# Attention heads with the gated branch's output products held behind their scores, two tiles a head, and the next head's loads written ahead

## The chip, the cores and the metric

The kernel runs on one core of one Trainium2 chip. Its time is device time in microseconds (us). A core has TensorE (PE, matrix products; its weight loads are shown apart as PEld), VectorE (DVE), ScalarE (ACT), GpSimd (POOL) and SyncE (SP), whose queue issues the kernel's transfers here. Each works through its own instructions in order, and they wait for each other by semaphores.

## What is computed

One decoder block on x of 1024 rows by 1024 columns, float32: half of the mixing width is attention with a forget gate in 8 heads of 64, the other half a gated branch in chunks of 128 rows; both go through one output matrix, then comes a gated feed-forward with a short convolution.

```
q, k, v, u, vg, f = split(rmsnorm(x) @ w_in)
logits = q @ k.T / 8 + c_i - c_j          # c: running sum of log sigmoid(f), causal
att = softmax(logits) @ v                  # 8 heads of 64
sg = u * (tril(w_s) @ rmsnorm(vg) + b_s)   # u, vg after gelu; 8 groups of 64, chunks of 128 rows
h = x + concat(att, sg) @ w_out
h = h + conv_ffn(rmsnorm(h))               # 1024 -> 2 x 2816 -> 1024, convolution of width 3
out = rmsnorm(h)
```

## The kernel before, in words

Products are made in float32r with each operand split into a high and a low part, so that one product of matrices is three on TensorE (high by high, high by low, low by high). The stages follow each other: input projections, attention, the output matrix, the up projection, the down projection. The program is written out in full; a scheduler then sets the order of each engine's instructions. It takes, of those that are ready by its own reckoning, the one that stands first in the program, and gives out buffers (each tag has a fixed number of them) as they come free. A helper, `after`, adds an order between two instructions of one engine without a wait. So the place of a piece in the program is its rank, and not its time.

The attention runs over 8 heads (`att_head`). A head loads five blocks into two tiles: A (queries, high and low part), B and B2 (keys, and the keys with their parts swapped), and nck, the forget sums laid over all partitions (L706 to L710). Tags "x1" and "x2" have two buffers, so a head's loads need the buffers of the head before the last. Then come four steps `i` of two query tiles `j` of 128 rows. For each `j` POOL forms the bias t (L725), TensorE the scores in "s" banks of PSUM (L733, L734, and the causal mask L736 on the diagonal), DVE adds both and takes the least (L738), ACT takes the exponent (L741). After the two `j` come as many tiles of the gated branch's products as `FILLS` says for this step, by `next(filler)`. Then the step's weights are transposed (L755), split in two by ACT and DVE (L756, L757) and multiplied with the values (L765). At the head's end its row sums are transposed (L777), stored and read back over 64 partitions (L779, L780). After each second head, POOL scales the pair's result and ACT and POOL split it into attT (L786 to L788); the third and the fourth pair's attT lie in "G" buffers.

The generator `sg_out` makes the gated branch's part of the output matrix: for each half of 512 columns it loads and splits four blocks of rows into the four "whl" buffers (L796 to L799), then, for each of 8 tiles of 128 rows, it loads x, makes twelve products of 128x512 into one bank (L808 to L810), adds x on DVE (L811) and stores the sum to hpd (L812). That is 16 tiles of twelve. Its left operands sgT fill all four "G" buffers until the last tile is done. The tiles' x and the raw weights share four "raw" buffers.

`wo_load` stands before the last head in the program. It loads the attention's four blocks of rows of the output matrix (L822) and splits them on ACT and POOL (L157 and L163 within `split_w`): the first two into the "whl" buffers, the other two into "G". After the heads come those rows' products (L906 to L908) and, with loads L865 and L881 into "raw" and sums on POOL (L884 to L887), the first weights of the up projection.

Of the kernel before, what the change touches and what calls it, by code (L numbers as in the profile page):

```python
# [16 lines left out]
BIG = 3.0e38  # L17
NFF = 22
WARM = 11
FILLS = [1, 2] * 10 + [2] + [0] * 11  # L20
FCFG = ("b", 4, 4)


# [35 lines left out]
def after(tc, later, earlier):  # L59
    tc.add_manual_dep(later.ins, earlier.ins.name, mybir.DependencyInfo(  # L60
        mybir.DependencyClass.NoSync, mybir.DependencyReason.DATA), reason="order")
# [3 lines left out]
def block_kernel(ctx: ExitStack, tc: tile.TileContext, xT, xtok, wuv, wv, wqk, wf, cpk, bfv,  # L65
                 ggain, g2r, gfr, wsp, woa, wos, wup, wdn, out):
    nc = tc.nc
    act, dve, pool, pe, sp = Line(nc.scalar, tc), Line(nc.vector, tc), Line(nc.gpsimd, tc), nc.tensor, nc.sync
# [6 lines left out]
    drm = ctx.enter_context(tc.tile_pool(name="drm", bufs=1, space=bass.MemoryType.DRAM))  # L75
    FILL = FILLS
    FTAG, FB, BB = FCFG
# [4 lines left out]
    def nm(s):  # L82
        uid[0] += 1
        return f"{s}_{uid[0]}"
# [18 lines left out]
    def f32(ap):  # L103
        return ap.bitcast(F32)
# [165 lines left out]
    B = [bank() for _ in range(4)]  # L270
# [61 lines left out]
    B, S = S, B  # L332
# [5 lines left out]
    for j in range(2):  # L338
        t1, t2, t3 = tmp[j]
        for c in range(2):  # L340
            k = 2 * j + c
# [27 lines left out]
    for j in range(2):  # L369
        t2 = tmp[j][1]  # L370
        for c in range(2):
            k = 2 * j + c
# [253 lines left out]
    for hf in (1, 0):  # L626
        for c in range(4):
            src = vgt[hf][:, :, c * P:(c + 1) * P].rearrange("p t (g d) -> p g t d", g=2)
            h = vgs[c][:, 0, :, hf * 4:hf * 4 + 4, :]
# [22 lines left out]
    sgT = [None] * 4  # L652
# [44 lines left out]
    attT = [None] * 4  # L697
    attF = [None] * 4

    TTAG = ["t01", "t01", "t2", "t3"]  # L700

    def att_head(h, order=(0, 1, 2, 3)):
        p, hh = h // 2, h % 2
        ab, nb = sb("x1", [P, 2, 1024], F32R), sb("x2", [P, 2, 1024], F32R)
        A, B, nck, B2 = ab[:, 0, :], ab[:, 1, :], f32(nb[:, 0, :]), nb[:, 1, :]
        sp.dma_start(out=f32(A), in_=qd[h].rearrange("s d t -> (s d) t"))  # L706
        sp.dma_start(out=f32(B), in_=kd[h].rearrange("s d t -> (s d) t"))
        sp.dma_start(out=nck, in_=ncd[h:h + 1, :].to_broadcast((P, 1024)))
        sp.dma_start(out=f32(B2[0:64, :]), in_=kd[h, 1])
        sp.dma_start(out=f32(B2[64:128, :]), in_=kd[h, 0])  # L710
        if hh == 0:
            attF[p] = sb("H", [P, 2, 1024])
        rs = sml.tile([P, 8], F32, tag="rs", name=nm("rs"))
        po = None
        tlow = sb("H", [P, 10 * P])
        for i in order:
            w1, w2 = (2 * i + 1) * P, (2 * i + 2) * P
            tp = tlow[:, 3 * i * P:3 * i * P + w1 + w2] if i < 2 else sb(TTAG[i], [P, w1 + w2])
            tj = (tp[:, 0:w1], tp[:, w1:w1 + w2])
            for jj in range(2):  # L720
                j = 2 * i + jj
                n = (j + 1) * P
                qs = slice(j * P, (j + 1) * P)
                t = tj[jj]
                pool.tensor_scalar(out=t, in0=nck[:, 0:n], scalar1=-1.0, scalar2=ncq[:, h, j:j + 1],  # L725
                                   op0=ALU.mult, op1=ALU.add)
                mn = sml.tile([P, 2], F32, tag="mn", name=nm("mn"))
                lo_ = lim[:, 0:1]
                for c in range(0, n, 512):
                    e = min(n, c + 512)  # L730
                    last = e == n
                    ps = sbank()
                    pe.matmul(ps[:, 0:e - c], A[:, qs], B[:, c:e], start=True, stop=False)  # L733
                    pe.matmul(ps[:, 0:e - c], A[:, qs], B2[:, c:e], start=False, stop=not last)  # L734
                    if last:
                        pe.matmul(ps[:, e - c - P:e - c], identb, maskb, start=False, stop=True)  # L736
                    m = mn[:, c // 512:c // 512 + 1]
                    dve.tensor_tensor_reduce(out=t[:, c:e], in0=ps[:, 0:e - c], in1=t[:, c:e], scale=1.0,  # L738
                                             scalar=lo_, op0=ALU.add, op1=ALU.min, accum_out=m)
                    lo_ = m  # L740
                act.activation(t, t, AF.Exp, bias=lo_, scale=-1.0, accum_out=rs[:, j:j + 1])  # L741
            for _ in range(FILL[4 * h + list(order).index(i)]):
                next(filler, None)
            if i % 2 == 0:
                po = bank()
            oc = (i % 2) * 256
            for k0 in range(0, 2 * i + 2, 2):
                pt = sb("pt", [P, 2, 512], F32R)
                ptr = bank()
                diag = k0 == 2 * i  # L750
                blocks = [(k0, 0, 0), (k0, 1, 128)] + ([(k0 + 1, 1, 256)] if diag else
                                                      [(k0 + 1, 0, 256), (k0 + 1, 1, 384)])
                w = 384 if diag else 512
                for k, jj, c in blocks:
                    pe.transpose(ptr[:, c:c + P], tj[jj][:, k * P:(k + 1) * P], ident)  # L755
                act.copy(pt[:, 0, 0:w], ptr[:, 0:w])  # L756
                dve.tensor_tensor(out=pt[:, 1, 0:w], in0=ptr[:, 0:w], in1=f32(pt[:, 0, 0:w]), op=ALU.subtract)  # L757
                for k in (k0, k0 + 1):
                    lhs = V[k // 2][:, k % 2, h, :, :].rearrange("p s d -> p (s d)")
                    half = k == 2 * i + 1  # L760
                    o = (k - k0) * 256
                    n = 128 if half else 256
                    oo = oc + (128 if half else 0)
                    for s in range(2):
                        pe.matmul(po[:, oo:oo + n], lhs, pt[:, s, o:o + n], start=(k == 0 and s == 0),  # L765
                                  stop=(s == 1 and half))
            if i % 2 == 1:
                hf = i // 2
                o = slice(hf * 512, hf * 512 + 512)
                r = slice(hh * 64, hh * 64 + 64)  # L770
                act.copy(attF[p][r, 0, o], po[64:128, :])
                dve.tensor_tensor(out=attF[p][r, 0, o], in0=po[0:64, :], in1=attF[p][r, 0, o], op=ALU.add)

        ptr = bank()
        rt = sb("t01", [8, P])
        dve.reciprocal(rs, rs)
        pe.transpose(ptr[0:8, 0:P], rs, ident)  # L777
        act.copy(rt, ptr[0:8, 0:P])
        sp.dma_start(out=rsd[h], in_=rt)  # L779
        sp.dma_start(out=attF[p][hh * 64:hh * 64 + 64, 1, :],  # L780
                     in_=rsd[h].rearrange("a b -> (a b)").unsqueeze(0).to_broadcast((64, 1024)))
        if hh == 1:
            attT[p] = sb("A" if p < 2 else "G", [P, 2, 1024], F32R)
            f = attF[p]
            for o, eng in (((slice(0, 1024), pool),) if p < 3 else ((slice(0, 512), dve), (slice(512, 1024), dve))):
                eng.tensor_tensor(out=f[:, 0, o], in0=f[:, 0, o], in1=f[:, 1, o], op=ALU.mult)  # L786
                act.copy(attT[p][:, 0, o], f[:, 0, o])
                eng.tensor_tensor(out=attT[p][:, 1, o], in0=f[:, 0, o], in1=f32(attT[p][:, 0, o]), op=ALU.subtract)  # L788

    def sg_out():  # L790
        for hf in range(2):
            o = slice(hf * 512, hf * 512 + 512)
            whs = []
            for kp in range(2):
                wr = sb("raw", [P, 2, 512])
                sp.dma_start(out=wr, in_=wos[hf, kp])  # L796
                for j in range(2):
                    w = sb("whl", [P, 2, 512], F32R)
                    split_w(wr[:, j, :], (w[:, 0], w[:, 1]), "act", "pool")  # L799
                    whs.append(w)  # L800
            for tt in range(8):
                ts_ = slice(tt * P, (tt + 1) * P)
                hs = sb("raw", [P, 512])
                sp.dma_start(out=hs, in_=xtok[ts_, o])
                ps = fbank()
                for k in range(4):
                    w = whs[k]
                    pe.matmul(ps, sgT[k][:, 0, ts_], w[:, 0, :], start=(k == 0), stop=False)  # L808
                    pe.matmul(ps, sgT[k][:, 0, ts_], w[:, 1, :], start=False, stop=False)  # L809
                    pe.matmul(ps, sgT[k][:, 1, ts_], w[:, 0, :], start=False, stop=(k == 3))  # L810
                dve.tensor_tensor(out=hs, in0=ps, in1=hs, op=ALU.add)  # L811
                sp.dma_start(out=hpd[tt, :, o], in_=hs)  # L812
                yield
# [5 lines left out]
    def wo_load():  # L819
        for k in range(4):  # L820
# [9 lines left out]
                w = [t[:, :, hf * 512:hf * 512 + 512] for hf in range(2)]  # L830
            wo.append(w)

    for h in range(8):
        if h == 7:
            for _ in filler:
                pass
            wo_load()
        att_head(h)


    ss2 = cst.tile([P, 8], F32, name="ss2")
# [129 lines left out]
    for tt in (0, 4, 1, 5, 2, 6, 3, 7):  # L971
        hload(tt)
        for hf in range(2):
# [3 lines left out]
            else:  # L977
                ps = bank()
# [29 lines left out]
    for i in range(AHEAD):  # L1008
# [4 lines left out]
        if i == 0:  # L1013

            last = flip(7)
# [311 lines left out]
```

## Time and profile before

| | |
|---|---|
| time, median of 3 runs | 1108.23 us (1107.27 to 1109.26) |
| the profiled execution's own time | 1112.15 us |
| its span, first to last instruction | 1110.4 us |
| granted TensorE clock, mean | 0.991 |
| busy: PE, DVE, ACT, POOL | 1079.6, 900.5, 572.3, 262.9 us |
| scores of head 0, first (L733) | at 226.5 us |
| gated branch's products (L808), first and last | at 233.1 and 314.2 us |
| first product of the attention's output rows (L906) | at 401.9 us |

A row of the profile names the engine, the line, what is written and read, how often, and how long. Line numbers are those of the kernel before. The clock is the share of full speed that TensorE was granted. A wait is put down to the instruction that ended it.

### The profile page before, as it was taken

What the parts mean: (1) busy time and instruction counts of PE and PEld (TensorE: products, weight loads), DVE (VectorE), ACT (ScalarE), POOL (GpSimd) and SP (SyncE); (2) the same over time, 40 slices, a digit from 0 to 9 for tenths busy, and PEclk for the clock granted to TensorE, in tenths of its full rate; (3) what the DMA queues carried; (4) which work ended last, traced back from release to release, by engine and by line L of the source; (5) the groups of instructions that cost most, each with busy time, mean ns of one, the idle gap of its engine ahead of it and who ended that gap; (6) DMA issues with size and microseconds to landing.
All of it is one profiled execution on the core that took longest, in us unless ns stands there. A gap on an engine that the chain in (4) does not pass through costs nothing.

```text
span 1110.4 us, 14553 instructions
## 1 busy us (share of the span) xinstructions
PE 1079.6 (97%) x5077; PEld 885.0 (80%) x5077; DVE 900.5 (81%) x1357; ACT 572.3 (52%) x990; POOL 262.9 (24%) x205
## 2 busy tenths in 40 slices
PE   9999998999998999998999999999999999999997
PEld 6888787787887788777788888888888888888886
DVE  5985799775668867799899999989898875898774
ACT  5656543454476775644444444353444445444653
POOL 0002233133245450243333332333242000000000
PEclk9999999999998999999999999999999999999999
DMA  9242356836575325322323133222321799433342
GB/s 339 82 152 77 97 165 175 256 126 216 188 210 165 105 100 185 114 72 81 114 95 123 67 123 114 95 96 104 133 80 54 254 321 333 135 95 96 125 139 97
DMA packets 64714, 158.19 MB, mean 142 GB/s; under 512 B 7672, under 2 KB 7936, under 8 KB 64640
## 3 DMA queue, kind: packets, MB, share of 16 engines
q1 hardware_dynamic: 64480, 156.73, 42.3%
q8 instruction: 40, 0.66, 0.2%
q10 hardware_dynamic: 160, 0.53, 0.1%
q14 instruction: 34, 0.28, 0.1%
HBM read 114.95 MB, written 42.27 MB: 142 GB/s over the span
## 4 chain that ended last, share of the span: by engine, by line
PE 68%; DVE 7%; ACT 3%; issue 2%; POOL 2%; DMA 1%; SPq 0%; ACTq 0%; DVEq 0%; POOLq 0%
PE k L1184 18%; PE qc L999 9%; PE qd L999 9%; PE qa L999 9%; PE qb L999 4%; PE pb L765 3%; PE ps L260 2%; PE pb L755 2%; PE pf L808 1%; PE pf L809 1%; PE pf L810 1%; DMA x<-ncd 1%; PE pb L906 1%; PE pb L908 1%; PE pb L907 1%
## 5 line engine op out<-in xcount | busy, mean ns | idle before, releaser
L1184 PE MATMUL k<-whb,wha 128*128 128x512 f32 x924 | 209.7, 389 | 0.0
L1184 PEld LDWEIGHTS k<-whb,wha 128*128 128x128 f32 x924 | 173.4, 188 | 36.1
L999 PE MATMUL qc<-xT,whb 128*128 128x512 f32 x540 | 132.0, 393 | 5.2 <-ACT cg L1078 3.1
L999 PE MATMUL qa<-xB,wha 128*128 128x512 f32 x528 | 127.2, 390 | 1.8 <-ACT xB L947 1.2
L999 PEld LDWEIGHTS qc<-xT,whb 128*128 128x128 f32 x540 | 102.2, 190 | 28.0 <-ACT cg L1078 3.5
L999 PEld LDWEIGHTS qa<-xB,wha 128*128 128x128 f32 x528 | 98.9, 188 | 22.7 <-ACT xB L947 1.5
L157 ACT CAST wha<-sg 128x512 fp32r<-128x512 f32 x77 | 47.9, 622 | 97.5 <-PE k L1184 85.5
L157 ACT CAST whb<-sg 128x512 fp32r<-128x512 f32 x88 | 53.8, 617 | 77.1 <-PE qc L999 70.0
L163 DVE TENSOR_TENSOR wha<-sg,wha 128x512 fp32r<-128x512 f32 x77 | 52.8, 688 | 42.1 <-ACT wha L157 41.9
L163 DVE TENSOR_TENSOR whb<-sg,whb 128x512 fp32r<-128x512 f32 x88 | 66.6, 759 | 9.4 <-ACT whb L157 9.3
L999 PE MATMUL qd<-xT,whb 128*128 128x512 f32 x264 | 63.7, 389 | 1.9 <-DVE u L1061 1.9
L999 PE MATMUL qd<-xB,whb 128*128 128x512 f32 x264 | 63.5, 390 | 0.4 <-DVE h L1071 0.4
L765 PE MATMUL pb<-pt,V 128*128 128x256 f32 (+1 forms) x320 | 59.8, 302 | 3.8 <-ACT pt L756 3.2
L756 ACT CAST pt<-pb 128x512 fp32r<-128x512 f32 (+1 forms) x80 | 41.2, 544 | 40.0 <-PE pb L755 39.5
L999 PE MATMUL qb<-xT,whb 128*128 128x512 f32 x252 | 61.0, 390 | 0.0
L885 POOL TENSOR_TENSOR sg<-sg,raw 128x512 f32<-128x512 f32 x22 | 44.0, 2000 | 68.8 <-issue 67.8
L999 PEld LDWEIGHTS qd<-xT,whb 128*128 128x128 f32 x264 | 49.5, 188 | 12.6 <-issue 2.3
L765 PEld LDWEIGHTS pb<-pt,V 128*128 128x128 f32 x320 | 48.0, 194 | 13.5 <-ACT pt L756 8.6
L999 PEld LDWEIGHTS qd<-xB,whb 128*128 128x128 f32 x264 | 49.5, 188 | 11.1 <-DVE h L1071 0.9
L757 DVE TENSOR_TENSOR pt<-pb,pt 128x512 fp32r<-128x512 f32 (+1 forms) x80 | 48.4, 633 | 11.9 <-ACT pt L756 11.5
L999 PEld LDWEIGHTS qb<-xT,whb 128*128 128x128 f32 x252 | 47.2, 188 | 10.1 <-DVE whb L163 0.4
L884 POOL TENSOR_TENSOR sg<-raw 128x512 f32<-128x512 f32 x22 | 29.4, 1335 | 101.0 <-DVE whb L163 94.6
(377 smaller groups left out, 2346.9 us busy)
## 6 DMA issues: line engine op xcount, KB each, us to landing
raw<-wup SPq DMA_DIRECT2D x44, 512.0 KB, 3.6
sg<-hx SPq DMA_DIRECT2D x77, 256.0 KB, 2.9
hx<-hs SPq DMA_DIRECT2D x44, 256.0 KB, 2.1
hx<-ca SPq DMA_DIRECT2D x33, 256.0 KB, 2.0
xT<-wdn SPq DMA_DIRECT2D x28, 256.0 KB, 4.4
raw<-wqk SPq DMA_DIRECT2D x8, 512.0 KB, 4.0
qd<-G SPq DMA_DIRECT2D x16, 256.0 KB, 3.9
kd<-G SPq DMA_DIRECT2D x16, 256.0 KB, 3.2
```

What stands on the lines that cost most here:

```text
L157: act.copy(h, src)
L163: return eng.tensor_tensor(out=l, in0=src, in1=f32(h), op=ALU.subtract)
L260: pe.matmul(banks[m], xs(n, xi, k)[:, ms], w[:, wi, :], start=(first and k == 0 and c == 0), stop=(k == 3 and c == 2), skip_group_check=True)
L755: pe.transpose(ptr[:, c:c + P], tj[jj][:, k * P:(k + 1) * P], ident)
L756: act.copy(pt[:, 0, 0:w], ptr[:, 0:w])
L757: dve.tensor_tensor(out=pt[:, 1, 0:w], in0=ptr[:, 0:w], in1=f32(pt[:, 0, 0:w]), op=ALU.subtract)
L765: pe.matmul(po[:, oo:oo + n], lhs, pt[:, s, o:o + n], start=(k == 0 and s == 0), stop=(s == 1 and half))
L808: pe.matmul(ps, sgT[k][:, 0, ts_], w[:, 0, :], start=(k == 0), stop=False)
L884: pool.tensor_tensor(out=s[0], in0=a21, in1=a22, op=ALU.add)
L885: pool.tensor_tensor(out=s[1], in0=s[0], in1=a11, op=ALU.add)
L999: pe.matmul(ps, w[:, wi, ks], xb[:, xi, k, :], start=(first and n == 0), stop=(n == 11), skip_group_check=True)
L1184: pe.matmul(banks[bk + m], xh[:, xi, ms], wh[:, wi, :], start=(first and p_ == 0 and n == 0), stop=(p_ == NP - 1 and n == 2), skip_group_c ...
```

## The change

Three edits in the attention, and no change to what is computed or to how many instructions of each kind there are, but for the order.

- `att_head` no longer issues its loads. A new function `att_load` does, and the loop over heads calls it for head h+1 ahead of `att_head(h)`. The loads so stand a whole head earlier in the program.
- `att_head` keeps the newest score product (the one with B2) in `place`. The first product of each tile of the gated branch is ordered behind it on TensorE.
- `FILLS` is now one tile at each of the four steps of the first head, then, counting heads from 0 as everywhere below, one at the second and one at the fourth step of heads 1 to 6, and none in head 7: 4 + 6 x 2 = 16. Before it was 1, 2, 1, 2 for each of the first heads until the 16 tiles were used up, which is in the third step of head 2.

```
-FILLS = [1, 2] * 10 + [2] + [0] * 11
+FILLS = [1] * 4 + [0, 1] * 12 + [0] * 4
...
+    place = [None]
...
-    def att_head(h, order=(0, 1, 2, 3)):
-        p, hh = h // 2, h % 2
+    def att_load(h):
         ab, nb = sb("x1", [P, 2, 1024], F32R), sb("x2", [P, 2, 1024], F32R)
...
+        return A, B, nck, B2
+
+    def att_head(h, ops, order=(0, 1, 2, 3)):
+        p, hh = h // 2, h % 2
+        A, B, nck, B2 = ops
...
-                    pe.matmul(ps[:, 0:e - c], A[:, qs], B2[:, c:e], start=False, stop=not last)
+                    place[0] = pe.matmul(ps[:, 0:e - c], A[:, qs], B2[:, c:e], start=False, stop=not last)
...
-                    pe.matmul(ps, sgT[k][:, 0, ts_], w[:, 0, :], start=(k == 0), stop=False)
+                    m = pe.matmul(ps, sgT[k][:, 0, ts_], w[:, 0, :], start=(k == 0), stop=False)
+                    if k == 0:
+                        after(tc, m, place[0])
...
+    ops = att_load(0)
     for h in range(8):
+        nxt = att_load(h + 1) if h < 7 else None
         if h == 7:
             for _ in filler:
                 pass
             wo_load()
-        att_head(h)
+        att_head(h, ops)
+        ops = nxt
```

## The prediction, made before the changed kernel ran

> **What bounds the kernel now.** I read the page first, then a table of stretches, then the waits, the DMA issues and the order of instructions inside the stretch that the change touches.
>
> ```profile
> span 1110.4 us, 14553 instructions
> PE 1079.6 (97%) x5077; PEld 885.0 (80%) x5077; DVE 900.5 (81%) x1357; ACT 572.3 (52%) x990; POOL 262.9 (24%) x205
> ```
>
> TensorE is busy 97% of the span, so an edit that moves the gated branch's products and adds none can win only what TensorE now loses inside the attention: idle time, and time at a lowered clock. The profiled execution took 1112.15 us, 3.9 above the median of 1108.23; I make the sum on its trace and carry the difference over.
>
> A head ends for TensorE with the transposition of its row sums (L777). The first fence has the row with the times of the first and the last; the second cuts the attention at all eight of them, one row a head, with the stretch behind it. Its columns are stretch, length, busy us of each engine, granted clock, DMA share and GB/s.
>
> ```profile
> L777 PE MATMUL pb<-ident,rs x8: 270/270/272, 263.0 to 410.6; 128*8 128x128 f32 x8
> ```
>
> ```profile
> 230.00:263.00 33.00, 32.91 (x188) 26.82 (x187) 21.76 (x50) 16.36 (x34) 6.20 (x11) 1.00 0.54 178
> 263.00:296.90 33.90, 33.08 (x183) 26.15 (x181) 18.61 (x43) 15.61 (x34) 9.18 (x10) 1.00 0.59 204
> 296.90:325.40 28.50, 28.40 (x172) 23.41 (x170) 18.67 (x50) 17.57 (x40) 15.62 (x14) 1.00 0.58 188
> 325.40:347.30 21.90, 18.61 (x116) 15.88 (x115) 15.81 (x44) 13.37 (x32) 5.86 (x8) 0.84 0.72 185
> 347.30:363.70 16.40, 15.91 (x113) 13.57 (x112) 14.91 (x41) 14.42 (x33) 12.27 (x14) 1.00 0.48 145
> 363.70:378.20 14.50, 13.86 (x101) 11.92 (x100) 11.94 (x33) 12.12 (x29) 4.62 (x6) 1.00 0.50 163
> 378.20:396.60 18.40, 16.11 (x120) 14.25 (x120) 14.38 (x39) 14.66 (x31) 13.86 (x12) 1.00 0.06 19
> 396.60:410.60 14.00, 13.51 (x95) 11.54 (x93) 10.99 (x27) 11.21 (x24) 8.23 (x7) 1.00 0.26 92
> 410.60:465.00 54.40, 52.46 (x259) 42.31 (x258) 41.88 (x65) 29.89 (x61) 4.51 (x3) 1.00 0.52 179
> ```
>
> Length less PE busy is idle time: 0.09, 0.82, 0.10, 3.29, 0.49, 0.64, 2.29 and 0.49 us in heads 0 to 7, together 8.2. Head 3 also ran at 0.84 of the clock, which is worth 0.16 x 21.9 = 3.5 us. So 11.7 us is all that a better order could win here, and 6.8 of it sits in head 3. The gated products (six tiles each in heads 0 and 1, four in head 2) are all over by then:
>
> ```profile
> L808 PE MATMUL pf<-whl,G x64: 388/393/504, 233.1 to 314.2; 128*128 128x512 f32 x64
> 242.52 0.39 PE L808 MATMUL pf<-whl,G 128*128 128x512 f32 x1
> 243.20 0.39 PE L808 MATMUL pf<-whl,G 128*128 128x512 f32 x1
> ```
>
> Three products take 0.68 us, so a tile of twelve takes 2.7 and all sixteen 44.
>
> **Why head 3 stalls.** Waits in its stretch, then what SyncE issued ahead of it, then one piece of the chain that ended last, and the last mask product of head 2:
>
> ```profile
> POOL H L725 <- DMA x<-ncd: 11.7, 1, 11.7
> DVE t L738 <- POOL t L725: 3.1, 1, 3.1
> PE ps L733 <- DVE mn L738: 2.0, 1, 2.0
> ...
> 313.23 3.41 SPq L822 DMA_DIRECT2D raw<-woa  x2
> 318.80 0.33 SPq L865 DMA_DIRECT2D raw<-wup  x1
> 319.20 0.41 SPq L706 DMA_DIRECT2D x<-qd  x1
> ...
> 320.12 11.87 DMA x<-ncd
> ...
> 319.01 0.23 PE L736 MATMUL ps<-maskb,identb 128*128 128x128 bf16 x1
> ```
>
> Head 4's operands are issued at 319.20, as soon as head 2's last score (319.01) gives up one of the two buffers. They come just behind loads for later stages (L822, L865; 128 x 1024 f32 each in the code, 512 KB) and take 11.87 us. Head 3, with no gated product left in it, is over before: POOL, then DVE, then TensorE wait for them. A stretch by tens shows what that does to the clock:
>
> ```profile
> 320.00:330.00 10.00, 9.76 (x74) 8.53 (x73) 8.68 (x27) 8.22 (x21) 0.45 (x1) 1.00 0.99 266
> 330.00:340.00 10.00, 6.96 (x42) 6.06 (x42) 6.43 (x17) 4.45 (x10) 5.86 (x8) 0.81 0.88 251
> 340.00:350.00 10.00, 9.99 (x65) 8.49 (x63) 7.33 (x24) 7.54 (x20) 2.13 (x2) 0.85 0.21 43
> 380.00:390.00 10.00, 8.26 (x59) 6.92 (x58) 8.00 (x22) 7.17 (x15) 5.55 (x6) 1.00 0.08 29
> ```
>
> 3.04 us idle in one ten, its longest wait 2.0, is followed by a lowered clock; 1.74 idle at 380 is not. [...]
>
> **The change, part by part.**
>
> *Holding each tile behind the newest score product.* It adds no instruction, only an order on TensorE. What now runs before that place? Head 1's first tile:
>
> ```profile
> 263.68 0.23 PE L736 MATMUL ps<-maskb,identb 128*128 128x128 bf16 x1
> 263.72 0.47 PE L808 MATMUL pf<-whl,G 128*128 128x512 f32 x1
> ```
>
> It already follows its tile's scores, at once. Price 0; it matters only where scores are late, and there a held tile can no longer fill the hole.
>
> *Two tiles a head through the seventh.* The same 44 us, but 5.5 in each of heads 1 to 6. Heads 3 to 6 last longer (14.5 to 16.4 becomes about 20 to 22 us), so a load issued when a buffer comes free has a whole such head to land, against 11.87 us at its worst. Per head only two loads and two stores of the gated branch (128 x 512 f32, 256 KB each) go with it; the 512 KB loads of L822 and L865 need "raw" buffers that those tiles hold, and move to the end. So head 3's stall goes: 3.29 + 3.5, less the 0.5 that heads 4, 5 and 7 idle anyway, is a gain of 6.3. What is late next is DVE, 82% to 91% of the stretch in heads 4 and 5; a longer head relieves it. The switch to the second half of the matrix now falls between head 2's last tile and head 3's first, several us apart, instead of between two tiles in a row, which takes away head 1's wait:
>
> ```profile
> PE pf L809 <- POOL whl L163: 0.6, 2, 0.3
> ```
>
> Gain 0.7 (0.82 less 0.1). Head 6's 2.29 us I leave: its cause, ACT and POOL forming attT of the third pair, remains.
>
> *What is given back.* The four "whl" and four "G" buffers are free only after the last tile, which is now in head 6 and not head 2. The output rows' splits in wo_load, and attT of the third pair, wait for them:
>
> ```profile
> 313.74 5.04 POOL L163 TENSOR_TENSOR whl<-raw,whl 128x512 fp32r<-128x512 f32 x4 [2.48 <-ACT whl L157]
> ...
> 388.86 2.42 POOL L788 TENSOR_TENSOR G<-H,G 128x1024 fp32r<-128x1024 f32 x1
> 392.90 4.76 POOL L163 TENSOR_TENSOR G<-raw,G 128x1024 fp32r<-128x1024 f32 x2
> 397.63 2.14 POOL L725 TENSOR_SCALAR t<-x,ncq 128x896 f32<-128x896 f32 x2
> ...
> 292.82 0.40 PE L810 MATMUL pf<-whl,G 128*128 128x512 f32 x1
> ```
>
> L788 and the G splits already stand ahead of head 7's last bias pair (L725 at 397.63, 1.0 after head 6's end at 396.6). New there are the four whl splits, 5.04 us of POOL. A head's last tile ends 4.1 us before the head does (292.82 against 296.9), so if POOL took all of 2.42 + 5.04 + 4.76 = 12.2 first, the pair would start 12.2 - 4.1 = 8.1 after head 6's end, 7.1 later than now. The lower bound is 0: POOL has 18.40 - 13.86 = 4.5 us idle in head 6 now, and 5.5 more when that head is longer. I take 2.0, nearer to 0 because that room is twice the 5.04. A gain is excluded, since nothing there gets earlier. The wup loads and sums also come later; the stretch from 410.6 has POOL at 4.51 of 54.40 us, and hides them. Without that cover 5 us would be at stake.
>
> *Next head's loads ahead in the program.* Five loads move past the head's row-sum store and reload, and past the gated branch's loads and stores, all on SyncE. They can't start earlier than a buffer comes free, so the gain is 0 beyond what is counted. The cost is that a load waiting at SyncE's head holds up those behind it:
>
> ```profile
> SPq L706 <- PE ps L736: 7.4, 5, 3.5
> ```
>
> Five such waits, 3.5 at the longest, exist already; behind them wait stores, and loads for tiles that are half a head from use. Price 0, at most 3.5 once.
>
> Sum: -6.3 - 0.7 + 2.0 = -5.0 us, 1107.2 for the profiled execution and 1103.2 for the median. From what was left open it reaches from -7.0 to +0.1, and with one 3.5 at SyncE to +3.6.
>
> **Rivals.** *All of it goes* (chance 0.12): the spread tiles also cover what I left in, and the whole 11.7 us is won: 1096.5. For it: idle time is spread over all of heads 3 to 7, where nothing fills. Against it: waits for ACT's copies (L756) cost heads with tiles in them as well.
>
> *The move only moves* (0.10): less its tiles (6, 6, 4 of 2.7), a filled head lasts 16.8, 17.7 and 17.7 us; the five unfilled ones last 17.0 on average with the stall in. If 17.4 is simply a head's price when tiles stand in it, eight of them and 44 make 183, against 180.6 from 230 to 410.6 now; with holds that do nothing this is 0 to +2, say 1109. Against it: the first window holds work of the stage before, and the third some scores of head 3.
>
> *The last head starves* (0.36), the slower side: head 7 has no tile to fill it, and POOL takes all splits first. The pair at L725 comes 7.1 us later, DVE can't empty the four score banks, and TensorE has neither scores nor output products to run; over 3 us idle in one ten halves the clock as in head 3, 3.5 more. 7.1 + 3.5 - 7.0 = +3.6, 1112. It decides once POOL's pair starts over 3.5 us later than now (with the clock) or 7 (without). For it: POOL works in order and wo_load stands before head 7 in the program. Against it: attT and the G splits stood there too, and head 7 still idled only 0.49.
>
> **How the numbers follow.** The forecast has 0.42. 0.2% is 2.2 us, about what a measurement can tell. Faster by more: 0.12 and nearly all of 0.42, 0.53. Slower by more: nearly all of the starved head and a little of the second, 0.36. Within: 0.11. Faster and slower both have weight, so the range reaches from the first rival's 1096.5 to a little past the third's 1112, 1113.5; the forecast's own is 1101.2 to 1108.
>
> **What would show it.** Right: no wait of POOL for ncd over 3 us in heads 3 to 6, a clock of 1.00 from 230 to the end of head 6, L808's products over six heads more, attention some 5 us shorter. Wrong in the given-back step: TensorE idle over 2 us and a lowered clock in the last head, with POOL at L163 just before L725. Wrong in the whole: stretches of filled heads that cost 2 us each more than their tiles.

## The result, and the profile after

The changed kernel takes 1113.95 us (median of 5 executions, 1112.64 to 1116.38), the kernel before 1108.57 beside it: a ratio of 1.0051 (95% interval 1.0036 to 1.0065), 5.4 us slower by the two medians. The forecast was 5.0 us faster. The profiled execution took 1115.87 us against 1112.15 before. Head of the page of the changed kernel:

```profile
span 1114.1 us, 14544 instructions
PE 1082.3 (97%) x5077; PEld 885.8 (80%) x5077; DVE 899.3 (81%) x1357; ACT 571.6 (51%) x990; POOL 263.6 (24%) x205
```

The number of products is the same; PE's busy time grew by 2.7 us, in part because products at a lowered clock last longer (a 128x512 product of L741 took 0.78 us at 402.90, where the clock was 0.50, and 0.39 at 405.31, where it was 1.00; 1.7 us more of clock is lost in the attention, as counted below). The attention, cut as in the prediction at the end of each head's row-sum transposition (now L784), columns as there (stretch, length, busy us of PE, PEld, DVE, ACT and POOL, clock, DMA share, GB/s):

```profile
230.00:257.90 27.90, 27.19 (x165) 22.30 (x163) 20.25 (x47) 17.35 (x37) 8.07 (x10) 1.00 0.41 141
257.90:280.80 22.90, 22.39 (x143) 18.67 (x143) 16.73 (x45) 14.01 (x34) 5.86 (x8) 1.00 0.61 187
280.80:304.00 23.20, 22.55 (x139) 17.97 (x138) 16.31 (x42) 16.12 (x37) 13.82 (x15) 1.00 0.47 148
304.00:325.00 21.00, 20.61 (x134) 17.06 (x132) 15.31 (x39) 12.69 (x29) 7.66 (x8) 1.00 0.59 189
325.00:350.90 25.90, 22.95 (x137) 18.89 (x136) 16.00 (x41) 14.61 (x33) 12.71 (x15) 0.93 0.47 143
350.90:372.40 21.50, 21.20 (x134) 17.26 (x133) 15.33 (x40) 12.68 (x30) 3.74 (x5) 1.00 0.51 171
372.40:394.10 21.70, 21.46 (x137) 17.53 (x135) 15.17 (x41) 15.72 (x33) 14.20 (x13) 1.00 0.25 75
394.10:415.10 21.00, 17.51 (x106) 15.44 (x104) 11.82 (x29) 12.29 (x25) 13.20 (x10) 0.84 0.47 150
```

The attention ends at 415.1 instead of 410.6, 4.5 us later. Over the eight heads, idle time grows from 8.2 to 9.2 us and the clock lost from 3.5 to 5.2 (0.07 x 25.9 + 0.16 x 21.0); the other 1.8 us is busy time at the full clock, which I can't place. Heads of different numbers of tiles compare once 2.7 us is taken off for each tile of twelve (before: 6, 6, 4 and none; after: 4, then 2 in each of heads 1 to 6, none in head 7):

| head | before, less tiles | after, less tiles | difference |
|---|---|---|---|
| 0, 1, 2 | 16.8, 17.7, 17.7 | 17.1, 17.5, 17.8 | +0.3, -0.2, +0.1 |
| 3 | 21.9 | 15.6 | -6.3 |
| 4 | 16.4 | 20.5 | +4.1 |
| 5 | 14.5 | 16.1 | +1.6 |
| 6 | 18.4 | 16.3 | -2.1 |
| 7 | 14.0 | 21.0 | +7.0 |

Head 3 gave the forecast 6.3. Heads 4 and 7 took it back and more. (A us or two of work can cross a cut from one head to the next, so I read nothing into head 5 alone: its idle time is 0.3 us, and 12 of the score products of L740 fall into it, against 8 of the same products, L733, before.) Both show a lowered clock and some 3 us of idle TensorE (25.90 - 22.95 and 21.00 - 17.51). The waits in them that the rest of this section follows, first one of head 4, then two of head 7:

```profile
POOL H L793 <- DVE pt L764: 5.5, 1, 5.5
```

```profile
ACT G L157 <- DMA raw<-woa: 3.6, 1, 3.6
PE pb L772 <- ACT pt L763: 3.4, 1, 3.4
```

**Head 4.** From the timeline of the changed kernel (start, us, engine, line, what, and in brackets the idle time before it):

```profile
327.35 0.29 SPq L786 DMA_DIRECT2D rsd<-t  x1
329.54 0.45 SPq L787 DMA_DIRECT2D H<-rsd  x1
333.02 2.39 POOL L793 TENSOR_TENSOR H<-H 128x1024 f32<-128x1024 f32 x1 [5.54 <-DVE pt L764]
335.44 1.04 ACT L794 CAST A<-H 128x1024 fp32r<-128x1024 f32 x1 [2.93 <-POOL H L793]
337.00 0.93 ACT L748 ACTIVATE t<-t,mn 128x768 f32<-128x768 f32 x1
338.08 0.55 PE L762 MATMUL pb<-ident,t 128*128 128x128 f32 x3 [2.82 <-ACT t L748]
```

Here POOL scales the second pair's result (L793), which needs the row sums of head 3 stored and read back (L786, L787). Behind POOL stands ACT, whose next instruction is the cast of that result (L794); the exponents that head 4 needs (L748) stand behind the cast, though nothing ties them to it. TensorE runs out of weights to transpose. The releaser that the profile names for POOL is an operation of DVE; the reload is what I read as the wait, issued 3.5 us before POOL starts, which is also the time that the profile gives from issue to landing for these reloads, and named as such for the same step before:

```profile
353.43 2.38 POOL L786 TENSOR_TENSOR H<-H 128x1024 f32<-128x1024 f32 x1 [3.98 <-DMA H<-rsd]
...
355.01 1.15 ACT L741 ACTIVATE t<-t,mn 128x1024 f32<-128x1024 f32 x1
356.15 1.03 ACT L787 CAST A<-H 128x1024 fp32r<-128x1024 f32 x1
```

In these rows of the kernel before, POOL waited 4 us as well, but ACT had its cast behind the last exponent and stood for nothing. That is where the order of instructions differs.

**Head 7**, from the timeline, and then the piece of the chain that ended last:

```profile
393.05 0.33 SPq L831 DMA_DIRECT2D raw<-woa  x1
397.20 1.04 ACT L157 CAST G<-raw 128x1024 fp32r<-128x1024 f32 x1 [3.56 <-DMA raw<-woa]
397.78 2.13 POOL L732 TENSOR_SCALAR t<-x,ncq 128x896 f32<-128x896 f32 x2
398.15 0.47 ACT L763 CAST pt<-pb 128x384 fp32r<-128x384 f32 x1
398.67 0.58 PE L772 MATMUL pb<-pt,V 128*128 128x256 f32 x1 [3.41 <-ACT pt L763]
```

```profile
391.73 1.31 POOL whl L163
393.05 4.12 DMA raw<-woa
```

The fourth block of the output rows needs a "raw" buffer, and the last one comes free only when POOL has split an earlier block (391.73 + 1.31). So its load starts at 393.05 and takes 4.12 us; ACT, in order, stands 3.56 us at the block's cast, ahead of the copy of weights (L763) that TensorE needs next. In stretches of one us the clock is 0.50 from 398 to 404 us and 1.00 again from 405 on; over the head that costs 0.16 x 21.0 = 3.4 us.

### The profile page after: what moved, and what is told of

Read it like the earlier page. It is cut to its first block, busy times and chain, and to the rows that moved or that the text cites. A ratio compares the mean times of both kernels' runs of the same rounds, so it can differ in the third digit from the quotient of the medians.

```text
span 1114.1 us, 14544 instructions
## 1 busy us (share of the span) xinstructions
PE 1082.3 (97%) x5077; PEld 885.8 (80%) x5077; DVE 899.3 (81%) x1357; ACT 571.6 (51%) x990; POOL 263.6 (24%) x205
## 4 chain that ended last, share of the span: by engine, by line
PE 69%; DVE 7%; ACT 3%; issue 3%; POOL 2%; DMA 0%; ACTq 0%; POOLq 0%; DVEq 0%
PE k L1196 18%; PE qc L1011 9%; PE qd L1011 9%; PE qa L1011 9%; PE qb L1011 4%; PE pb L772 3%; PE pb L762 3%; PE ps L260 2%; PE pf L815 1%; PE pf L818 1%; PE pf L819 1%; DVE whb L163 1%; PE pb L918 1%; PE pb L919 1%; PE pb L920 1%
## 5 line engine op out<-in xcount | busy, mean ns | idle before, releaser
L163 DVE TENSOR_TENSOR wha<-sg,wha 128x512 fp32r<-128x512 f32 x77 | 52.8, 688 | 41.6 <-ACT wha L157 41.5
L163 DVE TENSOR_TENSOR whb<-sg,whb 128x512 fp32r<-128x512 f32 x88 | 66.6, 758 | 9.4 <-ACT whb L157 9.3
L763 ACT CAST pt<-pb 128x512 fp32r<-128x512 f32 (+1 forms) x80 | 40.9, 543 | 48.1 <-PE pb L762 45.8
L764 DVE TENSOR_TENSOR pt<-pb,pt 128x512 fp32r<-128x512 f32 (+1 forms) x80 | 48.5, 634 | 17.3 <-ACT pt L763 17.1
L732 POOL TENSOR_SCALAR t<-x,ncq 128x896 f32<-128x896 f32 (+3 forms) x32 | 32.0, 1012 | 93.9 <-PE pb L762 63.7
```

The costliest lines, as they stand in the source:

```text
L163: return eng.tensor_tensor(out=l, in0=src, in1=f32(h), op=ALU.subtract)
```

## The experiments

Each ratio is against the kernel before, on the same chip, with its 95% interval; 0.0010 is 1.1 us. Diffs are against the changed kernel.

**Old places of the tiles, with the hold and the early loads kept.**

```
-FILLS = [1] * 4 + [0, 1] * 12 + [0] * 4
+FILLS = [1, 2] * 10 + [2] + [0] * 11
```

> The changed kernel with the old FILLS; the loads stay a head ahead in the program, and the hold stays. Theory A (the spread of the tiles over seven heads makes the loss, because the output rows' buffers come free only in head 6): gated tiles end near 314 us again, no stall in head 7, time within 2 us of the kernel before, 1107 to 1110. Rival B (the loads a head ahead push stores and row-sum reloads back on SyncE's queue, and that makes the loss): about 1112 to 1114, with waits for the reload of the row sums as in the changed kernel.

Measured: 1107.85 us, 1.0000 (0.9981 to 1.0018). Head 3 and head 7 are again those of before:

```profile
325.90:347.50 21.60, 18.62 (x116) 15.90 (x114) 15.67 (x42) 13.37 (x32) 5.83 (x8) 0.84 0.66 183
395.80:409.90 14.10, 13.60 (x97) 11.66 (x95) 11.10 (x29) 11.34 (x24) 8.25 (x7) 1.00 0.26 92
```

So the spread of the tiles makes the loss, and the other two edits together cost nothing that the interval of 2 us either way shows. No run takes the hold out alone; but the scheduler writes out the same order of instructions on all five engines with the hold and without it, at either set of places, so it does nothing.

**The loads back at their place.**

```
-        nxt = att_load(h + 1) if h < 7 else None
+        ops = None
...
-        att_head(h, ops)
+        att_head(h, att_load(h))
```

> The changed kernel with each head's loads back at the head itself; new FILLS and hold stay. Theory A: the stall of head 7 behind the last block of output rows stays, 1112 to 1115. Rival B: back to the kernel before, 1107 to 1110.

Measured: 1113.0 us, 1.0036 (1.0023 to 1.0049). Both stalls are there, first that of head 4, then that of head 7, where PE's wait is nearly the same to the tenth:

```profile
ACT A L794 <- POOL H L793: 4.3, 1, 4.3
PE pb L762 <- ACT t L748: 4.2, 1, 4.2
```

```profile
ACT G L157 <- DMA raw<-woa: 3.4, 1, 3.4
PE pb L772 <- ACT pt L763: 3.3, 1, 3.3
```

The early loads are not the cause.

**The last two blocks of output rows in buffers of their own,** so that their loads need no "raw" buffer.

```
-            wr = sb("raw", [P, 1024])
+            wr = sb("raw" if k < 2 else "wy", [P, 1024])
```

> The changed kernel with the raw form of the output rows' third and fourth block in the two wy buffers, which nothing uses any more, and not in raw, so that both loads land long before the last gated tile ends. Theory A1 (ACT stands 3.6 us at the cast of the fourth block, whose load waited for a raw buffer, and with it the copies that TensorE needs; 3.4 us idle, then the clock at half for 6.8 us, worth 3.4): both go, about 6 us less, 1106 to 1109, and the clock is 1.00 in head 7. Rival A2, the prediction's mechanism (POOL's last bias pair behind all splits starves the last head): POOL has the same work in the same order, so at most 1 us is won, 1112 to 1114.

Measured: 1112.47 us, 1.0028 (1.0013 to 1.0042), 2.5 us better than the changed kernel where about 6 was expected; the time alone lies where the rival, POOL's queue, had put it. Heads 4 and 7:

```profile
323.70:350.30 26.60, 22.66 (x136) 18.60 (x134) 15.94 (x41) 14.55 (x33) 12.64 (x14) 0.94 0.43 141
393.60:411.60 18.00, 16.35 (x107) 13.12 (x106) 11.79 (x29) 11.71 (x26) 13.30 (x10) 1.00 0.37 117
```

ACT's wait for the load is gone, the clock stays at 1.00, and head 7 falls from 21.0 to 18.0, not to 14 or 15. The expectation missed because a second limit stood right behind the first. POOL, with the splits no longer waiting, does all of them before the last bias pair:

```profile
397.36 2.39 POOL L163 TENSOR_TENSOR G<-wy,G 128x1024 fp32r<-128x1024 f32 x1
399.74 2.11 POOL L732 TENSOR_SCALAR t<-x,ncq 128x896 f32<-128x896 f32 x2
```

That pair starts 6.1 us after head 6's end at 393.6, and 5 us later, against that end, than before (1.0). That is the prediction's third rival, but second in line. In the changed kernel itself the pair starts at 397.78, 3.7 us after head 6's end.

**The pair's scaling and split in the last step of the next head,** ACT's cast ordered behind that step's last exponent.

```
+            if i == 3 and pend:
+                pend.pop()(ex)
...
-        if hh == 1:
+        def pair(ex):
...
+                if ex is not None:
+                    after(tc, m, ex)
...
+        if hh == 1 and p < 3:
+            pend.append(pair)
```

> The changed kernel in which a finished pair's scaling and split are written into the next head's last step, ACT's cast ordered behind that step's last exponent. Theory C (in head 4 ACT stands 2.9 us at the cast of the second pair's result, waiting for POOL, which waits for the reload of the row sums; TensorE idles 2.8 us and the clock halves for 3.4 us): both go from head 4, about 4 us less, 1108.5 to 1111, head 7 as in the changed kernel. Rival D (TensorE would have waited there anyway for the exponents, since head 4 is bound by POOL's late bias): less than 1.5 us, 1112.5 to 1114.

Measured: 1110.63 us, 1.0015 (1.0000 to 1.0029). Head 4 falls from 25.9 to 20.3 us with nothing idle, and head 7 keeps its stall:

```profile
324.20:344.50 20.30, 20.25 (x130) 16.83 (x129) 14.33 (x37) 12.45 (x27) 11.11 (x12) 1.00 0.53 168
388.80:408.40 19.60, 16.27 (x106) 14.28 (x105) 11.68 (x29) 12.20 (x25) 13.29 (x10) 0.91 0.50 161
```

So the place of the pair's work made head 4's stall. The edit moves POOL's scaling and split along with ACT's cast and doesn't tell them apart; that the cast stood in the way is read from the rows of head 4 above.

**Both cures** (the diffs of the two experiments before).

> The changed kernel with both cures: the rows' third and fourth raw block in the wy buffers, and the finished pair's cast behind the next head's last exponent. Theory E (the two stalls of ACT are two causes that add up, and with them gone the spread wins what was forecast): no clock below 1.00 from head 1 to head 7, 1103 to 1107. Rival F (a cure moves the wait to POOL's bias pair in head 7): head 7 idles 1 to 2 us more than in the old order and the time stays at 1108 to 1110, no better than the kernel before.

Measured: 1107.93 us, 0.9989 (0.9978 to 1.0000). The two add up: 0.0036 and 0.0023 below the changed kernel alone, 0.0062 together, which agree within the intervals. The time lies between the two expectations; head 7 stays at the 18.0 us of the third experiment, 1.65 of them idle, as the rival had it:

```profile
389.70:407.70 18.00, 16.35 (x107) 13.12 (x105) 11.77 (x29) 11.68 (x26) 13.31 (x10) 1.00 0.39 117
```

**Both cures, and the last two blocks' low parts on DVE instead of POOL.**

```
-                split_w(wr, (t[:, 0], t[:, 1]), "act", "pool")
+                split_w(wr, (t[:, 0], t[:, 1]), "act", "dve")
```

> As the run with both cures, with the low parts of the rows' third and fourth block made by DVE and not by POOL (4.76 us of POOL become about 2.4 of DVE). If POOL's queue still holds head 7 (rival F), its last bias pair comes 4 to 5 us earlier and 1 to 2 us are won on the run with both cures. If not (theory E), within 1 us of it.

Measured: 1106.84 us, 0.9970 (0.9958 to 0.9981), 3.3 us faster than the kernel before and the best version of this study. POOL's pair starts 2.2 us after head 6's end, and head 7 has 0.14 us idle:

```profile
389.70:405.80 16.10, 15.96 (x103) 12.96 (x102) 12.81 (x30) 11.54 (x24) 9.44 (x8) 1.00 0.42 128
391.93 2.12 POOL L732 TENSOR_SCALAR t<-x,ncq 128x896 f32<-128x896 f32 x2
```

POOL's queue was worth 18.0 - 16.1 = 1.9 us of that head. (In the trace before, an operation from 128x1024 f32 to fp32r took 1.23 us on DVE, L43 `V<-G,V`, and 2.41 on POOL, L163 `G<-raw,G`.)

**The same move to DVE alone, without the cures:** the prediction's mechanism taken away by itself.

> The changed kernel with nothing but those two low parts on DVE. Theory A1 (ACT waits for the fourth block's load, 3.4 us of TensorE and the half clock): the wait stands as it is, 1112.5 to 1115. Rival A2 (the prediction's, POOL's queue before the bias pair starves head 7): the pair comes over 4 us earlier and head 7 is 4 us shorter, 1108 to 1111.

Measured: 1116.2 us, 1.0060 (1.0044 to 1.0076), no better than the changed kernel. POOL is free, its pair starts 1.2 us after head 6's end (396.9), and TensorE waits 3.4 us for the copy of weights all the same:

```profile
398.11 2.11 POOL L732 TENSOR_SCALAR t<-x,ncq 128x896 f32<-128x896 f32 x2
399.66 1.04 ACT L157 CAST G<-raw 128x1024 fp32r<-128x1024 f32 x1 [4.39 <-DMA raw<-woa]
```

So in the changed kernel ACT behind a load, and not POOL's queue, starves the last head. The time lies above the 1112.5 to 1115 expected for this; why is open.

**Can head 3's stall be cured without moving a tile?** Old places of the tiles, and the loads of the output rows ordered on SyncE behind the last load of head 5's operands, so that head 4's operands do not come in behind them.

```
+        m = sp.dma_start(out=f32(B2[64:128, :]), in_=kd[h, 0])
+        hl_.append(m)
...
-            sp.dma_start(out=wr, in_=woa[k])
+            after(tc, sp.dma_start(out=wr, in_=woa[k]), hl_[5])
```

> Old FILLS, loads a head ahead, and the loads of the output rows ordered on SyncE behind the loads of head 5, so that they, and the up weights that take their buffers, no longer run beside head 4's loads. Theory G (the stall of head 3 in the kernel before is made by those neighbours): ncd lands in under 8 us, the stall and its half clock go, 1102 to 1105. Rival H (head 4's loads have no time anyway, since their buffer comes free with head 2's last score and head 3 has no gated tile): the stall keeps at least half of its 3.0 us and the clock falls still, 1106 to 1109.

Measured: 1110.89 us, 1.0013 (1.0004 to 1.0023). Heads 3 and 4:

```profile
324.90:342.10 17.20, 16.00 (x114) 13.32 (x112) 14.54 (x42) 12.66 (x30) 5.91 (x9) 1.00 0.46 146
342.10:363.80 21.70, 16.96 (x106) 14.59 (x104) 13.72 (x35) 14.96 (x33) 17.25 (x18) 0.85 0.64 189
```

Head 3 falls by 4.7 us with its clock at 1.00, so the loads beside head 4's made the larger part of its stall, as the first theory had it. But head 4 grows by 5.3, which neither theory named: ACT stands 3.6 us at the cast of the second pair (L795 here), as in the changed kernel. **With the cast placed late as well,** by the diff of the fourth experiment:

> Old FILLS, rows' loads held behind head 5's loads, and the finished pair's cast behind the next head's last exponent. In the run with the rows held alone ACT stood 3.6 us in head 4 at the pair's cast, waiting for POOL, and the clock fell. Theory C (this cast on ACT, behind the row sums' reload, is the same trap under either FILLS): the 3.9 us of TensorE's wait and the half clock go, about 6 us less, 1103 to 1106. Rival H (heads without gated tiles stall on their own operands' loads): the wait comes back in head 4 or 5 as a wait for ncd, 1108 to 1111.

Measured: 1111.28 us, 1.0019 (1.0007 to 1.0030): no gain, so my theory that the cast's place alone carried this stall fell for this order. ACT still waits 3.6 us for POOL:

```profile
352.97 1.30 POOL L163 TENSOR_TENSOR whl<-raw,whl 128x512 fp32r<-128x512 f32 x1
354.25 0.81 POOL L733 TENSOR_SCALAR t<-x,ncq 128x640 f32<-128x640 f32 x1
355.02 2.35 POOL L796 TENSOR_TENSOR H<-H 128x1024 f32<-128x1024 f32 x1
357.39 1.04 ACT L797 CAST A<-H 128x1024 fp32r<-128x1024 f32 x1 [3.63 <-POOL H L796]
358.35 1.55 ACT L766 CAST pt<-pb 128x512 fp32r<-128x512 f32 x3
```

The pair's scaling (L796) starts as soon as POOL has done a split of the output rows and biases, so here POOL's own queue is late, and the copies of weights (L766), which TensorE waits for, stand behind the cast although the exponents no longer do. A cast behind those copies, or splits off POOL in this order, wasn't tried.

**What head 3's stall costs from one execution to the next.** The kernel before, three times more.

> The kernel before, unchanged; its order of work is that of the first trace. Open: executions of it take from 1106.3 to 1113.3 us, with mean clocks from 0.997 to 0.990, and the one profiled execution that the prediction rests on had 1112.15 and 0.991. Theory P: head 3's 2 us stall lowers the clock in some executions only; then an execution near 1107 with a mean clock of 0.995 or more shows head 3 at 1.00 and about 18 to 18.5 us long instead of 21.9, with the same idle time of about 3, and the 6.3 us forecast for that stall held for some executions and was about 2.8 for the others. Theory Q: the lowered clock belongs to the stall in every execution; then head 3 shows 0.84 and 21 to 22 us in this trace as well, whatever its time, and the executions differ elsewhere. If this trace has a clock of 0.991 or so, it tells the two apart only if head 3 is at 1.00.

> As the run before it: theory P, head 3 at a clock of 1.00 and 18 to 18.5 us long in an execution of mean clock 0.995 or more; theory Q, 0.84 and 21 to 22 us in each.

> As the two runs before it. Over all traces of the order before, theory P expects head 3's length to fall in two groups some 3.5 us apart, theory Q in one.

Measured: 1110.60, 1110.48 and 1111.32 us, one execution each. Head 3 in the three traces, in that order:

```profile
324.50:346.00 21.50, 18.80 (x117) 16.05 (x116) 15.84 (x43) 13.43 (x32) 5.89 (x9) 0.84 0.65 186
```

```profile
325.20:345.80 20.60, 17.28 (x116) 14.83 (x114) 15.59 (x42) 13.40 (x32) 5.86 (x9) 0.92 0.78 195
```

```profile
325.30:345.80 20.50, 17.57 (x117) 15.19 (x116) 15.72 (x44) 13.46 (x32) 5.93 (x9) 0.92 0.72 200
```

With the trace before (21.9, 0.84) and the first experiment (21.6, 0.84) these are five traces with the same tile places. The clock lost is 0.16 x 21.5 = 3.4 us in three and 0.08 x 20.5 = 1.6 in two, so neither theory is right as put: the loss varies, but by half, and none of the five shows 1.00. All five have a mean clock of 0.993 or less. Among the 35 executions of the kernel before that stand beside the first four experiments, of which no trace was kept, some took 1106.4 to 1107 us at 0.997, where at most 0.003 x 1107 = 3.3 us of clock is lost in the whole program. Whether head 3 loses any there stays open.

## Why the prediction was wrong, point by point

- **The hold, price 0, and the loads ahead, price 0:** right. The orders agree with and without the hold, and the first two experiments leave the loads within their intervals.
- **Head 3's stall goes, -6.3:** right in the trace: POOL waits for ncd no more in heads 3 to 6 (its waits for it, 7.1 and 2.0 us, now fall into heads 1 and 2, where TensorE idles 0.5 and 0.7), and the clock of head 3 is 1.00. That it agrees to the tenth is chance, since head 3 now also holds 23 of its score products (L740, L741) against 28 before. For the median it is too much, since other executions of the kernel before lose 1.6 us of clock there instead of 3.5. This is one likely reason why the loss is 5.4 us in the medians and 3.7 between the two traced executions.
- **The switch wait of head 1, -0.7, and head 6's 2.29 left:** head 1 idles 0.51 instead of 0.82 us and gained 0.2. Head 6's idle time went from 2.29 to 0.24, now that tiles stand in it: a gain of 2.1 that I had left out of the sum.
- **"What is given back", +2.0:** this step failed: head 7 lost 7.0. The place was right (the output rows' loads and splits now crowd the last head), but I counted only POOL's 5.04 us of splits and took room on POOL for cover. The price lay on ACT: a load whose "raw" buffer comes free late (393.05), a cast that waits for it, and a copy for TensorE behind the cast: 3.4 us of wait and 3.4 of clock. What I did price, the delay of POOL's last pair, came near: it starts 2.7 us later against head 6's end than before (3.7 against 1.0). (My 4.1 us from a head's last tile to its end should be 3.7, since 292.82 is where that product starts; the upper bound of this term grows by 0.4.) I had written that the loads "move to the end" and did not ask who stands in line behind their landing.
- **"What is late next is DVE":** failed too, and cost +4.1 in head 4, a loss that the sum put at nothing. DVE's share fell as I said, in heads 4 and 5 from 91% and 82% to 62% and 71%. What came late was POOL's scaling behind the reload of the row sums, with ACT's cast of it now ahead of head 4's exponents.
- **The rivals.** *The last head starves* forecast 1112 by POOL's queue; the time came near and all its signs appeared (idle over 2 us and a lowered clock in the last head, L163 at 396.53 just before the pair). But its own condition, a pair over 3.5 us later than before, was not met with 2.7, and the move to DVE alone shows that the mechanism was another, and that POOL's queue is worth 1.9 us only once ACT's wait is gone. *The move only moves* fell: net of tiles heads 3, 5 and 6 cost 15.6 to 16.3, and head 4 without its stall 20.3 - 5.4 = 14.9, not 17.4. *All of it goes* was right for heads 3, 5 and 6, whose idle time is under 0.4 us, and wrong for heads 4 and 7.
- **The sum.** With the two stalls cured and POOL relieved the attention ends at 405.8, 4.8 us earlier than in the trace before; I had forecast 5.0. Less their tiles, heads 0 to 3 gain the 7.0 us of the first two terms there, and heads 4 to 7 give back 2.2 (head 7 alone 2.1, of which 0.14 is idle). That the last is close to my 2.0 is chance: I had priced POOL's queue, and in this version two splits are off POOL; with them on it, in the run with both cures, head 7 gives back 4.0. In the medians that version gains 3.3.

## What to carry over

When work is spread to cover one stall, follow every buffer that it now holds longer to the loads that need it, and from each load to the in-order engine that will stand at its landing: the price is what waits behind that instruction, not the instruction's own time. Look where a conversion stands whose input comes through a store and a reload: a scheduler that goes by rank may place it ahead of work that the next stage needs once a neighbouring stage changes length. Placing it later won about 4 us here with the tiles spread, and nothing with the tiles at their old places and the loads held. And take more than one trace before a lowered clock is booked to a stall in full.

## What the hardware did that I had not expected

The clock fell in the changed kernel after a single wait of 2.82 us. Stretches of ten around the two stalls, and one of a single us behind the second:

```profile
335.00:345.00 10.00, 7.08 (x34) 5.67 (x34) 6.45 (x19) 7.87 (x18) 6.22 (x8) 0.83 0.78 223
395.00:405.00 10.00, 6.59 (x30) 5.93 (x29) 4.25 (x12) 6.04 (x13) 8.12 (x6) 0.66 0.80 258
398.00:399.00 1.00, 0.33 (x1) 0.33 (x2) 0.35 (x1) 1.00 (x4) 1.00 (x2) 0.50 1.14 311
```

The first lost 1.7 us (0.17 of 10), the second, after 3.41 us of wait, 3.4. The 18.00 - 16.35 = 1.65 us that head 7 idles, in pieces under 1 us, with the output rows in buffers of their own cost no clock at all. And one order of instructions lost 1.6 or 3.4 us at one and the same stall from one execution to the next. In stretches of one us the lowered clock reads 0.50: from 337 to 342 us in the trace before, and from 340 to 343 and from 398 to 404 in that of the changed kernel. So the losses of 1.7 and 3.4 us are about 3.4 and 6.8 us at half the clock: in these traces the loss comes in two sizes, one double the other. Why one and the same stall costs now 1.6 and now 3.4 us, no trace shows.
